# First layer's scale and shift as column-group products on TensorE instead of dot products on VectorE

## The chip, the cores and the metric

The kernel runs on one core of a Trainium2 chip. The metric is the device time of one execution in microseconds (us), the median of several runs. Engines: PE is TensorE (PEld its weight loads), DVE is VectorE, ACT is ScalarE, POOL is GpSimd, SP issues most of the loads.

## What is computed

Three layers over 256 positions of width 1024, all in float32: an attention layer (`nsa`), a dilated attention layer, and a block with two feed-forward parts and a gated delta mixer. Each layer is preceded by a norm whose scale and shift (and, behind it, whose gate) come from a conditioning row `c` by a large product. Cut to what the change touches:

```python
def adaln_norm(x, c, g, w_ada, b_ada):
    mod = jax.nn.silu(c) @ w_ada + b_ada            # c: (1, 1024), w_ada: (1024, 3072)
    shift, scale, gate = jnp.split(mod, 3, axis=-1)
    h = rms_norm(x, g) * (1.0 + scale[:, None, :]) + shift[:, None, :]
    return h, gate[:, None, :]

# first layer
h, gate = adaln_norm(x, c, norm_g[0], ada_w[0], ada_b[0])
u = h @ nsa_w_in[0]                                 # then the attention
```

So no column of the first layer's big product `h @ w_in` can start before the scale and shift of its 1024 features are there: 2 x 1024 dot products of length 1024, 8 MB of weights.

## The kernel before

All weights come as "units" of 1 MB (128 partitions x 2048 floats), one DMA each, issued by SP in the order in which the program fetches them (`fetch`, L235), into a ring of three buffers named `raw`. A load waits until its buffer's last reader is done. A weight unit of a product (`unit`, L241) is split by ACT into a rounded `hi` and by DVE into the rest `lo` (`split`, L218), and `part` (L288) multiplies hi and lo with the hi and lo halves of the activations, three passes a weight block, through `mm` (L208; every matmul of the kernel has its line L209).

An `ada` unit holds the weights of 256 output features, transposed so that a feature lies on a partition. DVE makes each as a dot product along the row: one `scalar_tensor_tensor` with `accum_out` over 128x1024 for every 128 features (L374), against the row silu(c) that stands in all partitions (`scrow`, made by `silu_row` with two PE broadcasts); one small addition adds the bias (L377). `ada_gen` is a generator, `self.step(n)` runs n units of it.

The stretch of the change is `first` (L713). It goes through the 1024 features in four steps u = 0 to 3 of 256 features. Each step runs two `ada` units (shift and scale of these 256 features), forms `a` = (1 + scale) g (L725), applies the norm to two 128-feature blocks (`apply_to`: DVE L597, ACT L600, DVE L601), and multiplies them with one weight unit, 48 matmuls of 128x256 on PE into four PSUM banks. After u = 1 and u = 3 comes one more unit (48 matmuls) for further columns. That makes 14 units: in each step two `ada` units and a weight unit, and the two extra ones. When the last step is through, the evacuations begin (`ev_kv` first), with copies and rotations on ACT, DVE and POOL, and the attention follows.

A scheduler sets the order of instructions on each engine beforehand; on the chip each engine runs its own list in order. PSUM has eight banks by tag: three `g`, two `s`, two `t`, one `o`; in `first` the four step accumulators take g, g, g, s, the extra columns s and t.

The trace also holds another stretch that the prediction reads: the compression of keys and values, L843 to L862. There `o` <- `raw`,`ke` is a float32 product with 32 columns of PE for each of eight 128-row blocks, in four column groups (`p = slice(32 * (m % 4), ...)`), `hidt` is its copy out of PSUM, and `t` <- `id`,`hidt` folds the four groups into one with a small matmul. A float32 matmul shows as two PE instructions.

Of the kernel before, what the change touches and what calls it, by code (L numbers as in the profile page):

```python
# [11 lines left out]
AF = mybir.ActivationFunctionType  # L12
ALU = mybir.AluOpType
# [130 lines left out]
def pack_units(inp, plan):  # L144

    ws = np.zeros((NUNIT, 128, 2048), np.float32)
    assert len(plan) == NUNIT
    for u, (kind, name, idx, a, b, cols) in enumerate(plan):
        w = np.asarray(inp[name])[idx]
        if kind == "gemm":  # L150
            blk = np.concatenate([w[a * 128:(a + b) * 128, c0:c0 + wd] for c0, wd in cols], 1)
            n = blk.shape[1]
            ws[u, :, :b * n] = blk.reshape(b, 128, n).transpose(1, 0, 2).reshape(128, b * n)
        elif kind == "ada":
            ws[u] = w[:, a:a + 256].T.reshape(2, 128, 1024).transpose(1, 0, 2).reshape(128, 2048)
        else:
            ws[u] = w.reshape(16, 128, 256)[a:a + 8].transpose(1, 0, 2).reshape(128, 2048)
    return ws


class Net:
    def __init__(self, ctx, tc, A, out):
        self.tc, self.nc, self.A, self.out = tc, tc.nc, A, out
        self.n = 0
        self.plan = []
        self.fine = 0
        self.queue, self.ready, self.later = [], None, []
        self.layer = "n"
        self.want32 = False
        self.rate, self.credit = RN[0], -0.25  # L170
        self.C, self.sect = {}, {}
        P = lambda name, bufs, **kw: ctx.enter_context(tc.tile_pool(name=name, bufs=bufs, **kw))
        self.cp = P("cp", 1)
        self.praw = P("praw", 3)
        self.phi = P("phi", int(2*2048//HW))
        self.plo = P("plo", int(2*2048//HW))
        self.big = P("big", 11)
        self.tmp = P("tmp", 2)
        self.ps = P("ps", 1, space=PSUM)
        self.dram = P("dram", 1, space=bass.MemoryType.DRAM)  # L180
# [182 lines left out]
    def ada_gen(self, jobs):  # L363
        nc = self.nc
        sc2 = None
        for name, idx, sc, mod, j, us, bias in jobs:
            if sc is None:
                sc = sc2 = sc2 or self.silu_row(self.A["c_2"])
            for u in us:
                raw = self.fetch("ada", name, idx, j * 1024 + u * 256, 0, None)  # L370
                for k in range(2):
                    r = raw[:, k * 1024:(k + 1) * 1024]
                    n = j * 8 + 2 * u + k
                    nc.vector.scalar_tensor_tensor(r, r, 1.0, sc, op0=ALU.mult, op1=ALU.mult, accum_out=mod[:, n:n + 1])  # L374
                if u == us[-1]:
                    o = slice(j * 8 + 2 * us[0], j * 8 + 2 * u + 2)
                    nc.vector.tensor_tensor(mod[:, o], mod[:, o], bias[:, o], op=ALU.add)  # L377
                    self.done.add((id(mod), j))
                yield

    def step(self, n=1):
        for _ in range(n):
# [11 lines left out]
    def setup(self):  # L394
        nc, A = self.nc, self.A
        v8 = lambda x: x.rearrange("p (k t) -> p k t", k=8)
        self.small = self.t(self.cp, [128, NSMALL])
        self.eps = self.t(self.cp, [128, 1])
        nc.vector.memset(self.eps, EPS)
        self.eps2 = self.t(self.cp, [128, 1])  # L400
        nc.vector.memset(self.eps2, EPS * EPS)
        self.ones = self.t(self.cp, [128, 128])
        nc.vector.memset(self.ones, 1.0)
        c = self.b8()[0:1, :1024]
        nc.sync.dma_start(c, A["c"])
        x = self.b8()
        self.xT = v8(x)
        nc.sync.dma_start(self.xT, A["xT"])
        self.consts(self.cp, "base")
        sq = self.b8()  # L410
        for h in range(2):
            nc.scalar.activation(sq[:, h * 1024:(h + 1) * 1024], x[:, h * 1024:(h + 1) * 1024], AF.Square)
        sc = self.silu_row(c, True)
        nc.sync.dma_start(self.small, A["small"])

        self.mod = [self.t(self.cp, [128, 24]), self.t(self.cp, [128, 24]), self.t(self.cp, [128, 72])]
        jobs = []
        ab, b2 = self.vec("ada_b"), self.vec("b_ada_2")
        all4 = range(4)
        for l in range(2):  # L420
            js = [(j, [u]) for u in all4 for j in range(2)] + [(2, all4)] if l == 0 else [(j, all4) for j in range(3)]
            jobs += [("ada_w", l, sc, self.mod[l], j, us, ab[:, l * 24:l * 24 + 24]) for j, us in js]
        jobs += [("w_ada_2", 0, None, self.mod[2], j, all4, b2) for j in range(9)]
        self.done = set()
        self.bg = self.ada_gen(jobs)
        self.ident, self.one = self.C["ident"], self.ones
        for n in (1024, 512, 256)[:2]:
            nc.vector.tensor_tensor(sq[:, :n], sq[:, :n], sq[:, n:2 * n], op=ALU.add)
        n //= 256
        self.ss, f = self.bank("o"), None  # L430
        for kt in range(n):
            for q in range(2):
                i = self.mm(self.ss[:, q:q + 1], sq[:, kt * 256 + q * 128:kt * 256 + q * 128 + 128], self.ones[:, 0:1], f is None, kt == n - 1, f)
                f = f or i
        self.og = self.t(self.cp, [128, 8, 2])
        self.mhalf = self.t(self.cp, [128, 16])
        nc.vector.memset(self.mhalf, -0.5)

    def silu_row(self, row, pe=False):

        nc = self.nc
        sc = self.t(self.cp, [128, 1024], tag="scrow")
        if not pe:
            nc.sync.dma_start(sc, row.to_broadcast([128, 1024]))
        for h in range(2):
# [5 lines left out]
            th = self.w([128, 512], tag="w5", bufs=4)  # L451
# [261 lines left out]
    def first(self, xT, W, ca, cb, cc, evacs):  # L713

        nc = self.nc
        mod, g = self.mod[0], self.vec("norm_g")
        r = self.rstd()
        h = [self.b8(F32R).rearrange("p (k t) -> p k t", k=8) for _ in range(2)]
        act = [(h[0][:, k], h[1][:, k]) for k in range(8)]
        a = self.w([128, 8], tag="acol")  # L720
        G = [self.group(512, tags=t) for t in ("gg", "gs", "st")]
        for u in range(4):
# [7 lines left out]
            if u in FD:  # L730
                cols = list(ca) + [cb]
                raw = self.fetch("gemm", W[0], W[1], 2 * u, 2, cols)
                for i in range(2):
                    self.direct(G[i], [raw[:, k * 1024 + i * 512:k * 1024 + i * 512 + 512] for k in range(2)], self.x32, 2 * u, 8)
            else:
                self.fine, self.last_sq = 1, None
                ws = self.unit(W, 2 * u, 2, list(ca) + [cb])
                for i in range(2):
                    c = slice(i * 512, (i + 1) * 512)
                    self.part(G[i], ws[i::2] if HW < 1024 else [(hi[:, c], lo[:, c]) for hi, lo in ws], act, 2 * u, 8, u < 3)  # L740
            if u % 2:
                if u // 2 in FC:
                    raw = self.fetch("gemm", W[0], W[1], 4 * (u // 2), 4, [cc])
# [3 lines left out]
                    self.part(G[2], ws, act, 4 * (u // 2), 8)  # L747
            if u == 2:
                self.consts(self.sp, "rope")
        for G, ev in zip(G, evacs):  # L750
            ev(G[0])
        return act

    def _nsa(self, xT):
# [3 lines left out]
        mod = self.mod[0]  # L758
# [150 lines left out]
        nc.vector.tensor_tensor(pc, pc, mx[:, :, :, None].to_broadcast([128, 2, 16, 16]), op=ALU.mult)  # L909
        self.fill(FN[5])  # L910
        self.step(AN[5])
        pct = self.w([128, 2, 256], tag="pct", bufs=1)
        b = self.bank("t")
        for g in range(2):
            for q in range(2):
# [790 lines left out]
```

## Time and profile before

| | us |
|---|---|
| median of 3 runs | 1101.57 |
| lowest and highest run | 1100.72, 1111.84 |
| the profiled execution | 1111.95 |
| span of its trace | 1110.2 |

| engine | busy us | share of the span |
|---|---|---|
| PE | 1055.9 | 95% |
| PE weight loads | 982.6 | 89% |
| DVE | 850.9 | 77% |
| ACT | 608.5 | 55% |
| POOL | 77.4 | 7% |

These shares are over the whole span; the stretch `first` is its first 62 us. Times in the rows below count from the start of the span. "Idle before" an instruction, in square brackets, is how long its engine stood still ahead of it, and what released it. The column PEclk is the granted TensorE clock, 1.00 being 2.4 GHz and 0.50 being 1.2 GHz.

### The profile page before, as it was taken

Reading aid. Unit: us, or ns where it says so; the run is one execution under the profiler, and the core shown is the slowest. Engines: PE = TensorE matmul, PEld = TensorE weight load, DVE = VectorE, ACT = ScalarE, POOL = GpSimd, SP = SyncE. Lnnn points to the kernel's source line nnn. Section 1 sums busy time; section 2 is a strip of 40 time slices with the busy share of each in tenths; the row PEclk is TensorE's granted clock in tenths of the full one; section 3 lists DMA queues with packets and bytes.
Section 4 is the critical chain, followed back from the end, with each engine's and each line's share of the span. In section 5 each row is a group of like instructions: output and inputs, shape, how many; then the busy total and the mean of one; then the engine's idle time right before and its main releaser. Section 6 shows DMA issues by size and latency. Waiting matters only on the chain.

```text
span 1110.2 us, 20852 instructions
## 1 busy us (share of the span) xinstructions
PE 1055.9 (95%) x8453; PEld 982.6 (89%) x8453; DVE 850.9 (77%) x1558; ACT 608.5 (55%) x1160; POOL 77.4 (7%) x94
## 2 busy tenths in 40 slices
PE   5879999989999999999999899999999999999997
PEld 4868767877789899999989788988899999999997
DVE  7987997998999998877798876678666776655543
ACT  3483776787665644544487256526445565444442
POOL 0030000221000000000003121310010000000000
PEclk9988999999999999999999889999899999999999
DMA  8965575575967588887744524273356545555451
GB/s 315 337 226 206 190 265 180 189 241 200 322 223 299 184 297 302 296 301 275 285 153 146 121 84 145 83 221 113 101 173 223 187 156 162 180 191 170 172 190 38
DMA packets 34577, 225.99 MB, mean 204 GB/s; under 512 B 4897, under 2 KB 5185, under 8 KB 8498
## 3 DMA queue, kind: packets, MB, share of 16 engines
q1 hardware_dynamic: 31826, 219.88, 55.7%
q0 software_dynamic: 2368, 4.27, 1.9%
q8 instruction: 66, 1.08, 0.4%
q10 hardware_dynamic: 288, 0.52, 0.1%
q14 instruction: 29, 0.24, 0.1%
HBM read 223.34 MB, written 1.31 MB: 202 GB/s over the span
## 4 chain that ended last, share of the span: by engine, by line
issue 35%; PE 24%; ACT 3%; DVE 3%; DMA 1%; POOL 0%; POOLq 0%; DVEq 0%; ACTq 0%; SPq 0%
PE g L209 17%; PE s L209 5%; PE t L209 2%; PE o L209 1%; DVE w L1241 1%; DMA raw<-in_ws_dram 1%; ACT hi L219 1%; DVE lo L222 1%; DMA b<-dr 0%; ACT d L1322 0%; ACT b L599 0%; ACT b L600 0%; ACT d L1347 0%; PE t L216 0%; DVE xt L1395 0%
## 5 line engine op out<-in xcount | busy, mean ns | idle before, releaser
L209 PE MATMUL g<-b,hi 128*128 128x256 f32 (+2 forms) x3696 | 697.5, 287 | 13.7 <-ACT b L600 8.5
L209 PEld LDWEIGHTS g<-b,hi 128*128 128x128 f32 (+1 forms) x3696 | 581.3, 191 | 22.6 <-ACT b L600 10.4
L209 PE MATMUL g<-b,lo 128*128 128x256 f32 (+2 forms) x1848 | 520.8, 287 | 4.3 <-DVE lo L222 4.2
L219 ACT CAST hi<-raw 128x1024 fp32r<-128x1024 f32 (+2 forms) x302 | 279.9, 953 | 250.7 <-PE g L209 127.1
L222 DVE TENSOR_TENSOR lo<-raw,hi 128x1024 fp32r<-128x1024 f32 (+2 forms) x302 | 329.5, 1113 | 92.4 <-ACT hi L219 89.8
L209 PEld LDWEIGHTS g<-b,lo 128*128 128x128 f32 (+1 forms) x1848 | 350.2, 192 | 8.2 <-DVE lo L222 6.6
L374 DVE SCALAR_TENSOR_TENSOR raw<-raw,scrow 128x1024 f32<-128x1024 f32 x120 | 144.8, 1227 | 8.0 <-DMA raw<-in_ws_dram 7.7
L209 PE MATMUL s<-b,hi 128*128 128x256 f32 (+1 forms) x288 | 64.0, 288 | 2.3 <-ACT w L560 2.3
L209 PE MATMUL s<-b,b 128*128 128x128 f32 (+2 forms) x224 | 49.7, 345 | 7.7 <-ACT w L691 3.1
L209 PE MATMUL g<-b,raw 128*128 128x256 f32 x208 | 52.7, 394 | 0.0
L209 PEld LDWEIGHTS s<-b,hi 128*128 128x128 f32 x288 | 49.5, 194 | 2.5 <-ACT w L560 2.5
L209 PEld LDWEIGHTS g<-b,raw 128*128 128x128 f32 x208 | 39.1, 198 | 5.9 <-issue 1.2
L209 PEld LDWEIGHTS s<-b,b 128*128 128x128 f32 x224 | 30.3, 192 | 15.1 <-issue 5.0
L1241 DVE SCALAR_TENSOR_TENSOR w<-pad,u,w 128x256 f32<-128x256 f32 x96 | 41.5, 476 | 1.0 <-ACT w L1236 0.9
L209 PE MATMUL s<-b,lo 128*128 128x256 f32 (+1 forms) x144 | 40.3, 287 | 0.0
L502 POOL TENSOR_TENSOR rcol<-rcol,u 128x2 f32<-128x2 f32 x5 | 3.5, 700 | 489.2 <-ACT rcol L501 489.2
L209 PE MATMUL t<-b,hi 128*128 128x256 f32 x160 | 37.5, 281 | 0.0
L1152 DVE TENSOR_TENSOR w<-w,g 128x512 f32<-128x512 f32 (+1 forms) x21 | 14.2, 674 | 24.8 <-PE g L209 24.8
L947 ACT ACTIVATE p<-s,mxs 128x256 f32<-128x256 f32 (+1 forms) x64 | 26.5, 422 | 7.9 <-DVE dens L950 6.6
L1150 ACT ACTIVATE w<-g 128x512 f32<-128x512 f32 (+1 forms) x21 | 12.3, 587 | 31.8 <-PE g L209 31.8
L209 PE MATMUL g<-hi,b 128*128 128x512 f32 (+1 forms) x96 | 28.7, 376 | 0.2 <-ACT w L691 0.2
L209 PEld LDWEIGHTS t<-b,hi 128*128 128x128 f32 x160 | 28.4, 188 | 0.0
(330 smaller groups left out, 1273.0 us busy)
## 6 DMA issues: line engine op xcount, KB each, us to landing
raw<-in_ws_dram SPq DMA_DIRECT2D x202, 1024.0 KB, 5.0
raw<-in_ws_dram SPq DMA_DIRECT2D x4, 512.0 KB, 5.3
b<-dr POOLq DMA_DIRECT2D x8, 256.0 KB, 6.6
raw<-in_ws_dram SPq DMA_DIRECT2D x2, 608.0 KB, 4.2
b<-in_xT_dram SPq DMA_DIRECT2D x1, 1024.0 KB, 4.9
b<-dr POOLq DMA_DIRECT2D x8, 128.0 KB, 4.1
u<-in_consts_dram SPq DMA_DIRECT2D x2, 384.0 KB, 5.0
b<-dr POOLq DMA_DIRECT2D x4, 192.0 KB, 10.1
```

What stands on the lines that cost most here:

```text
L209: i = self.nc.tensor.matmul(out, lhsT=lhsT, rhs=rhs, start=start, stop=stop, skip_group_check=True)
L219: i = self.nc.scalar.copy(hi, src)
L222: self.nc.vector.tensor_tensor(lo, src, hi, op=ALU.subtract)
L374: nc.vector.scalar_tensor_tensor(r, r, 1.0, sc, op0=ALU.mult, op1=ALU.mult, accum_out=mod[:, n:n + 1])
L502: nc.gpsimd.tensor_tensor(r, r, self.mhalf[:, 0:2], op=ALU.pow)
L947: nc.scalar.activation(p[:, br], sv[:, br], AF.Exp, bias=mx[:, q, br:br + 1], accum_out=den[:, q, br:br + 1])
L1150: nc.scalar.activation(t, gb, AF.Tanh, scale=0.5)
L1152: nc.vector.tensor_tensor(t, t, ub, op=ALU.mult)
L1241: nc.vector.scalar_tensor_tensor(dst, fl(pad[:, o:o + 256]), taps[i], dst, op0=ALU.mult, op1=ALU.add)
```

## The change

The eight `ada` units that `first` runs are no longer dot products on DVE. Their weights are packed the other way round (`adac`: the 1024 inputs on the partitions, in eight blocks, 256 output features along the row). silu(c) is put into a column tile `c4`: eight blocks of 32 columns, zero but for the first column of each. Eight float32 matmuls with `c4`'s blocks as the 32-column operand sum into four column groups of a PSUM bank `cbank` (m = 0..3 start the groups, m = 4..7 add to them). ACT copies the 128x256 result into SBUF (`hidt`), two matmuls against a column of ones fold the four groups and turn 256 features onto the partitions, into other columns of the same bank, and DVE adds the bias from there. The bank `cbank` is one of the two `t` banks. The row `scrow` is still made, since later units need it, but behind the first sum of squares.

```diff
         elif kind == "ada":
             ws[u] = w[:, a:a + 256].T.reshape(2, 128, 1024).transpose(1, 0, 2).reshape(128, 2048)
+        elif kind == "adac":
+            ws[u] = w[:, a:a + 256].reshape(8, 128, 256).transpose(1, 0, 2).reshape(128, 2048)
...
             for u in us:
+                if self.c4 is not None and len(us) == 1:
+                    self.ada_product(name, idx, mod, j, u, bias)
+                    self.done.add((id(mod), j))
+                    yield
+                    continue
                 raw = self.fetch("ada", name, idx, j * 1024 + u * 256, 0, None)
...
+    def ada_product(self, name, idx, mod, j, u, bias):
+
+        raw = self.fetch("adac", name, idx, j * 1024 + u * 256, 0, None)
+        b, n = self.cbank, j * 8 + 2 * u
+        for m in range(8):
+            p = slice(32 * (m % 4), 32 * (m % 4) + 32)
+            self.mm(b[p, :256], self.c4[:, m], raw[:, m * 256:(m + 1) * 256], m < 4, m >= 4, self.clast)
+        t = self.t(self.sp, [128, 256], tag="hidt", bufs=1)
+        self.nc.scalar.copy(t, b[:, :256])
+
+        for k in range(2):
+            self.clast = self.mm(b[:, 256 + n + k:257 + n + k], t[:, k * 128:(k + 1) * 128], self.ones[:, 0:1])
+        self.nc.vector.tensor_tensor(mod[:, n:n + 2], b[:, 256 + n:258 + n], bias[:, n:n + 2], op=ALU.add)
...
-        sc = self.silu_row(c, True)
         nc.sync.dma_start(self.small, A["small"])
+        sc = self.t(self.cp, [128, 1024], tag="scrow")
...
         n //= 256
+        self.silu_row(c, True, sc)
         self.ss, f = self.bank("o"), None
...
         act = [(h[0][:, k], h[1][:, k]) for k in range(8)]
+
+        c4, th = self.w([128, 512], tag="pct", bufs=1)[:, :256], self.w([128, 8], tag="acol")
+        self.c4 = c4.rearrange("p (k i) -> p k i", k=8)
+        nc.gpsimd.memset(c4, 0.0)
+        nc.scalar.activation(th, self.vec("c"), AF.Tanh, scale=0.5)
+        nc.vector.tensor_scalar(th, th, 1.0, 0.5, op0=ALU.add, op1=ALU.mult)
+        nc.vector.tensor_tensor(self.c4[:, :, 0], th, self.vec("c"), op=ALU.mult)
+        self.cbank, self.clast = self.bank("t"), None
         a = self.w([128, 8], tag="acol")
...
+        self.c4 = None
         for G, ev in zip(G, evacs):
```

What the scheduler makes of it on PE at the start of the program, behind the sums of squares (`o_113`), before the change (`o_135` is the norm factor spread over all partitions, `g_141` and `g_142` two of the accumulators of step u = 0):

```order
L209 MATMUL o_113<-u_4_83,b_8_91 128x1 x4
L209 MATMUL o_135<-u_7_89,rcol_132 128x128 x2
L209 MATMUL g_141<-b_30_138,hi_168 128x256 x2
L209 MATMUL g_142<-b_30_138,hi_168 128x256 x2
L209 MATMUL g_141<-b_30_138,lo_169 128x256 x2
```

and in the changed kernel at the same place (`t_146` is `cbank`, `pct_140` is `c4`, `raw_154` and `raw_169` the two units of step 0, `u_4_83` the ones):

```order
L212 MATMUL o_113<-u_4_83,b_8_91 128x1 x4
L212 MATMUL t_146<-raw_154,pct_140 32x256
L212 MATMUL o_135<-u_7_89,rcol_132 128x128 x2
L212 MATMUL t_146<-raw_154,pct_140 32x256 x7
L212 MATMUL t_146<-u_4_83,hidt_164 128x1 x2
L212 MATMUL t_146<-raw_169,pct_140 32x256 x8
L212 MATMUL t_146<-u_4_83,hidt_179 128x1 x2
L212 MATMUL g_148<-b_30_138,hi_195 128x256 x2
```

Twenty matmuls of the two units now stand on PE ahead of the first matmul of step 0, seven of the first eight products behind `o_135`.

PE at the border of steps 0 and 1, before the change (`hi_249` is the first half of step 1's weight unit):

```order
L209 MATMUL g_143<-b_31_139,hi_174 128x256 x2
L209 MATMUL s_144<-b_31_139,hi_174 128x256 x2
L209 MATMUL g_141<-b_30_138,hi_249 128x256 x2
L209 MATMUL g_142<-b_30_138,hi_249 128x256 x2
L209 MATMUL g_141<-b_30_138,lo_250 128x256 x2
```

and in the changed kernel (`raw_255` and `raw_270` are the two units of step 1, `hi_296` the first half of its weight unit):

```order
L212 MATMUL g_150<-b_31_139,hi_201 128x256 x2
L212 MATMUL s_151<-b_31_139,hi_201 128x256 x2
L212 MATMUL t_146<-raw_255,pct_140 32x256 x8
L212 MATMUL t_146<-u_4_83,hidt_265 128x1 x2
L212 MATMUL t_146<-raw_270,pct_140 32x256 x8
L212 MATMUL t_146<-u_4_83,hidt_280 128x1 x2
L212 MATMUL g_148<-b_30_138,hi_296 128x256 x2
```

All products of step 1's units stand behind the last matmul of step 0 and ahead of the first of step 1; the borders to steps 2 (there behind the 48 matmuls of the extra unit) and 3 look the same.

DVE ahead of step 1, before the change (L374 the dot products, L377 the bias, L725 `a`, L597 the norm's application, L222 the split):

```order
L222 TENSOR_TENSOR lo_175<-raw_166,hi_174 128x512 x2
L374 SCALAR_TENSOR_TENSOR raw_228,u_14_108<-raw_228,scrow_94 128x1024 x2
L377 TENSOR_TENSOR u_14_108<-u_14_108,u_1_78 128x2
L374 SCALAR_TENSOR_TENSOR raw_233,u_14_108<-raw_233,scrow_94 128x1024 x2
L377 TENSOR_TENSOR u_14_108<-u_14_108,u_1_78 128x2
L725 SCALAR_TENSOR_TENSOR acol_140<-u_14_108,u_1_78 128x2
L597 SCALAR_TENSOR_TENSOR xr_239<-b_6_87,acol_140,o_135 128x256
```

and in the changed kernel (L401 the bias, L756 `a`, L620 the application, L225 the split):

```order
L225 TENSOR_TENSOR lo_202<-raw_193,hi_201 128x512 x2
L401 TENSOR_TENSOR u_10_96<-t_146,u_1_78 128x2
L225 TENSOR_TENSOR lo_297<-raw_294,hi_296 128x512
L401 TENSOR_TENSOR u_10_96<-t_146,u_1_78 128x2
L225 TENSOR_TENSOR lo_297<-raw_294,hi_296 128x512
L756 SCALAR_TENSOR_TENSOR acol_147<-u_10_96,u_1_78 128x2
L225 TENSOR_TENSOR lo_303<-raw_294,hi_302 128x512
L620 SCALAR_TENSOR_TENSOR xr_286<-b_6_87,acol_147,o_135 128x256
```

The dot products are gone, and splits of step 1's weight unit have moved up between the bias and the application. At step 2 all splits stand ahead of the bias, at step 3 one stands behind the second bias. On SP three loads of constants (0.94 MB together) that came behind the last unit of `first` now stand ahead of step 3's three units and the extra one.

## Rows read from the trace of the kernel before

**Rows 1.** Busy time in stretches of the program: steps 0 to 3, then the rest

```profile
core 0: us, PE busy (x) PEld busy (x) DVE busy (x) ACT busy (x) POOL busy (x), PEclk, DMA share, GB/s
17.50:26.80 9.30, 8.43 (x49) 8.23 (x49) 9.16 (x20) 3.10 (x7) 0.00 (x0) 1.00 0.83 314
26.80:39.30 12.50, 11.78 (x96) 11.43 (x96) 11.54 (x22) 5.04 (x9) 0.00 (x0) 1.00 0.96 364
39.30:48.60 9.30, 6.14 (x48) 5.79 (x48) 9.16 (x20) 3.10 (x7) 0.00 (x0) 1.00 0.90 344
48.60:54.10 5.50, 5.39 (x25) 4.64 (x26) 5.47 (x11) 3.82 (x6) 0.00 (x0) 0.69 0.75 255
...
66.00:100.00 34.00, 26.73 (x193) 21.28 (x193) 27.30 (x46) 21.63 (x42) 5.22 (x5) 0.80 0.68 240
100.00:1110.00 1010.00, 978.65 (x7936) 915.70 (x7934) 768.13 (x1405) 556.19 (x1068) 65.44 (x79) 0.98 0.56 196
```

**Rows 2.** The chain that ended last, in order of time: its longest piece

```profile
907.47 195.46 issue
```

**Rows 3.** DVE in order of time ahead of step 1: start, duration, instruction

```profile
20.44 1.22 DVE L374 SCALAR_TENSOR_TENSOR raw<-raw,scrow 128x1024 f32<-128x1024 f32 x1
...
25.33 0.16 DVE L377 TENSOR_TENSOR u<-u,u 128x2 f32<-128x2 f32 x1
...
26.51 0.69 DVE L222 TENSOR_TENSOR lo<-raw,hi 128x512 fp32r<-128x512 f32 x1
```

**Rows 4.** PE in order of time: the first matmuls of steps 0 to 3

```profile
17.52 1.23 PE L209 MATMUL g<-b,hi 128*128 128x256 f32 x4 [2.07 <-ACT b L600]
...
26.80 0.74 PE L209 MATMUL g<-b,hi 128*128 128x256 f32 x4 [0.84 <-ACT b L600]
...
39.34 0.74 PE L209 MATMUL g<-b,hi 128*128 128x256 f32 x4 [0.76 <-ACT b L600]
...
48.62 0.39 PE L209 MATMUL g<-b,hi 128*128 128x256 f32 x1 [3.13 <-ACT b L600]
```

**Rows 5.** ACT in order of time: the norm ahead of step 1, a weight unit's first cast

```profile
26.24 0.91 ACT L600 ACTIVATE b<-xr,u 128x256 fp32r<-128x256 f32 x2
...
47.12 0.62 ACT L219 CAST hi<-raw 128x512 fp32r<-128x512 f32 x1 [5.87 <-DMA raw<-in_ws_dram]
```

**Rows 6.** Busy time in a stretch of 2 us, columns as in rows 1

```profile
18.00:20.00 2.00, 2.00 (x11) 2.00 (x11) 2.00 (x5) 1.42 (x3) 0.00 (x0) 1.00 1.04 434
```

**Rows 7.** PE in order of time: small matmuls of the start and the compression, one pause

```profile
11.21 1.87 PE L209 MATMUL o<-u,b 128*128 128x1 f32 x8 [5.14 <-DVE b L428]
14.23 1.22 PE L209 MATMUL o<-u,rcol 128*128 128x128 f32 x4 [1.15 <-POOL rcol L502]
...
67.61 1.07 PE L209 MATMUL o<-raw,ke 128*32 128x256 f32 x16 [1.58 <-DMA raw<-in_ws_dram]
...
74.97 1.93 PE L209 MATMUL o<-raw,ke 128*32 128x256 f32 x14
...
85.51 0.58 PE L209 MATMUL g<-b,lo 128*128 128x256 f32 x1 [1.24 <-DVE lo L222]
...
95.91 0.53 PE L209 MATMUL t<-id,hidt 128*128 128x32 f32 x4
```

**Rows 8.** ACT, costliest groups by shape: one copy of 128x256 out of PSUM

```profile
L970 ACT COPY b<-o 128x256 f32<-128x256 f32 x8 | 3.0, 376 | 5.2 <-PE o L209 5.1
```

**Rows 9.** PE alone in stretches: busy time, granted clock, DMA, in the compression

```profile
67.00:68.00 1.00, 0.39 (x8) 1.00 0.00 0
...
75.00:76.00 1.00, 1.00 (x12) 0.50 0.08 25
...
84.50:85.00 0.50, 0.00 (x0) 0.54 0.93 197
...
86.00:91.00 5.00, 5.00 (x25) 0.50 0.73 270
```

More of the change, by code (lines that the diff above doesn't have):

```diff
@@ L437, in setup, with silu_row @@
         nc.vector.memset(self.mhalf, -0.5)
-    def silu_row(self, row, pe=False):
+    def silu_row(self, row, pe=False, sc=None):
         nc = self.nc
-        sc = self.t(self.cp, [128, 1024], tag="scrow")
+        sc = self.t(self.cp, [128, 1024], tag="scrow") if sc is None else sc
         if not pe:
@@ L749, in first @@
                 self.consts(self.sp, "rope")
+        self.c4 = None
         for G, ev in zip(G, evacs):
@@ L911, in _nsa @@
         self.step(AN[5])
-        pct = self.w([128, 2, 256], tag="pct", bufs=1)
+        pct = self.w([128, 512], tag="pct", bufs=1).rearrange("p (g t) -> p g t", g=2)
         b = self.bank("t")
```

## The prediction

> **What bounds the kernel now.** I read the busy time by stretches first. From 100 us to the end PE is busy 978.65 of 1010 us [rows 1], and the longest piece of the chain of waits there is "issue" for 195.46 us [rows 2]: PE waits for nothing else. A shift of what comes before 100 us is therefore passed on to the end, and the change is worth what it does to `first`.
>
> In `first` two engines share the limit. DVE is busy 9.16 of 9.30 us in step 0 and 9.16 of 9.30 in step 2 [rows 1]: four dot products take 20.44 to 25.33 [rows 3]. PE is busy 8.43, 11.78 and 6.14 us in the same stretches and stands still only 0.84 us ahead of step 1, 0.76 ahead of step 2 and 3.13 ahead of step 3 [rows 4], because DVE's dot products run beside PE's matmuls of the step before. The loads come third: in the one wait for a weight unit shown, at 47.12, ACT stood still 5.87 us [rows 5], and the stretch moves 314 to 364 GB/s, where 434 are reached in 18 to 20 us [rows 1, 6].
>
> So PE has some 5 us of idle time at the borders of steps 0 to 3, and the reader should ask what is put into PE's list, and where.
>
> **What is removed.** Sixteen dot products, 4.9 us of DVE a step [rows 3], 19.6 us in all. They were hidden from PE but for the gaps above; what can come back from them is at most these gaps, 0.84 + 0.76 + 3.13 = 4.7 us, and the start.
>
> **What is added at a border.** By the order on PE, the products of a step's two units stand behind the previous step's last matmul, and each unit is a chain of its own: eight products, copy on ACT, fold on PE, bias on DVE. The first bias is ahead of the second unit's products, since both are in one bank. All of it is paid with PE's list held:
> - Eight products: the compression has the same shape, 128x32 weights against 128x256 in float32; sixteen PE instructions take 1.07 us at 67.61, where the granted clock is 1.00, and fourteen 1.93 us at 74.97, where it is 0.50 [rows 7, 9]. I take 1.0.
> - The copy: 0.376 us [rows 8], and two hand-overs of some 0.1: the first of two norm instructions ends at 26.24 + 0.91 / 2 = 26.70 [rows 5], PE starts on it at 26.80 [rows 4]. That is 0.55 to 0.6; I take 0.55.
> - The fold: four PE instructions, 0.53 us [rows 7]. I take 0.5.
> - The bias: 0.16 us [rows 3] and a hand-over: 0.25.
> - From the second bias to the first matmul: 25.33 to 26.80 [rows 3, 4] is 1.47, as before.
>
> Sum: (1.0 + 0.55 + 0.5 + 0.25) + (1.0 + 0.55 + 0.5 + 0.05) + 1.47 = 5.9 us. At step 1 two splits of 0.65 us (start to start; 0.69 alone, [rows 3]) stand in DVE's list between the bias and the application, at step 3 one: 7.2, 5.9 and 6.5 us in place of 0.84, 0.76 and 3.13. That is +6.4, +5.1 and +3.4, together **+14.9 us**.
>
> What is queued behind: the step's whole PE list, and the split's buffers. A product that comes later frees its `raw` buffer later, but the unit that then loads has a step of 12 us and more (5.9 to 7.2 and 6.14) ahead of it, so loads do not decide; the 0.95 MB of constants ahead of step 3's units cost 2.2 us of loading at 434 GB/s [rows 6] and are covered by the same time. If that cover were gone they would cost these 2.2 us. The zeroing of `c4`, its three small operations and the later `scrow` lie under the first loads.
>
> **The start.** `o_135` ends at 14.23 + 1.22 = 15.45 [rows 7], then seven products: fourteen instructions, to 17.4 if they take the slow 1.93 us. I take the slow durations up to step 0, since its 49 matmuls take 8.43 us against 6.14 for step 2's 48 [rows 1], though the clock column reads 1.00 for both. Copy 0.55; fold at the slow clock, half of the 1.87 us that eight instructions with one column took [rows 7], 0.93; bias 0.25; eight products 2.2; copy 0.55; fold 0.93; 0.05 and the 1.47 to the first matmul: 24.3 us, where it was 17.52 [rows 4]. **+6.8 us.**
>
> **The clock.** Step 0 took 8.43 us against 6.14 in step 2 [rows 1]. PE will have been active on and off since 11 us when step 0 starts at 24.3, so part of that loss goes: between 0 and 2.3 us, I take **-1.2**, as the last splits on DVE still end some 3.5 us behind the step's start. Step 3's first 25 matmuls took 5.39 us at a granted clock of 0.69 [rows 1], behind the 3.13 us pause [rows 4]. With the new borders PE never pauses as long: its pauses are 0.55, 0.25, 0.55 and 1.5 us. If the clock holds, step 3 gains 5.39 - 25 x 0.128 = **-2.2 us**. But in another place the clock fell in the course of a pause of only 1.24 us [rows 7], to 0.54 and 0.50, and 25 matmuls took 5.0 us instead of 3.2 [rows 9]; the pattern at the new borders is between the two. A fall costs 1.8 to 2.2 us, and there are three borders. I take one fall: **+2**.
>
> The Trainium skill (TensorE: Matmul & The Clock Gate, "A second HAM failure mode: psum-queue depth-cycling") says that short pauses of PE between groups of matmuls make the clock go back and forth between its two levels. If that held at every border, the sum would be 26, as the second rival says; the fall at 84.5 us agrees with it.
>
> **Sum.** 14.9 + 6.8 - 1.2 - 2.2 + 2 = **+20.3 us**. Behind `first` the evacuations start when the first group of step 3 is done; all engines wait for that, so the shift goes on. Against the profiled execution's 1111.95 us that is 1132; the shown runs' median is 1101.57, 0.9% below it, and as the sum is a difference I add it to the median: **1122 us**.
>
> **Rivals.**
> 1. *The loads decide, and they get faster* (the other side, not slower). Buffers that products read free early, the loads run without pauses: 17.5 to 48.6 us moved 9.3 x 314 + 12.5 x 364 + 9.3 x 344 = 10.7 MB [rows 1], 24.6 us at 434 GB/s [rows 6] in place of 31.1. Less 2.2 for the constants, a gain of 4.3: **1097 us**. For it: DVE's full stretches, ACT's 5.87 us wait. Against it: it needs the products to pass PE before the step that stands ahead of them, and PE's order has them behind. It decides only if a border's chain fits into the old gaps of 0.8 to 3.1 us; I get 5.9 to 7.2. Chance 0.05.
> 2. *The clock falls at every border.* Then step 0 and step 3 gain nothing, and steps 1 and 2 lose some 2.2 us each: 14.9 + 6.8 + 4.4 = +26, and with the products and folds there also at 0.50 (+0.9 and +0.4 a unit, six units) up to +34: **1128 to 1135 us**. Chance 0.20.
> 3. *The shift is partly absorbed.* Between 66 and 100 us PE is idle 34 - 26.7 = 7.3 us [rows 1]. If that idle time ends with loads or DVE work that do not move with `first`, or if a border's pieces overlap better than in series, up to 8 us come back and the clock holds: +8 to +12, **1110 to 1113 us**. Against it: the work there starts from step 3's accumulators. Chance 0.12.
> 4. *The four column groups do not run at once*, so that the change doesn't do what it says: sixteen instructions one after the other at no less than step 2's 0.128 us are 2.05 us in place of 1.0, eight times: +8 more, **1130 us** and up. Against it, the compression's 1.07 us [rows 7]. Chance 0.03.
>
> The Trainium skill (TensorEngine Tiling (Array Packing), "PSUM Bottleneck") warns that column groups speed up PE but not the copy out of PSUM, which may become the limit. The rows agree: the products take 1.0 us a unit, the copy and fold behind them 1.05 and more. By it alone (products free, the rest in series) a border would still cost 3.9 to 5.2 us.
>
> **How the numbers follow.** The forecast's own case, +13 to +25, has 0.60. The range leaves out rival 1, the top of 2, the upper part of 4 and the bottom of 3: 1110 to 1132. About 1% is what a measurement of this kernel can tell from no change, 11 us: faster than 1090.5 needs more than the loads give in rival 1, 0.03 of its 0.05; within 1% are the rest of it and most of rival 3, 0.12; slower than 1112.6 the rest, 0.85.
>
> **What the new profile would show.** Right: PE starts step 0 near 24 us, step 1 near 39, step 2 near 57 and step 3 near 69, with pauses released by ACT (the copy), DVE (the bias) and ACT (the norm) at each border; DVE idle in `first` for a third of the time and more; loads below 300 GB/s there; the same PE work from 100 us on, later by some 20 us. Wrong: pauses of PE that end with a load (then buffers, not the chain, decide), products that take over 2 us a unit at the granted 1.00, step 3 started before 60 us, or a shift at step 3 that is gone by 110 us. The clock's part can be read from the granted clock at the borders: 1.00 throughout takes 2 us off, 0.50 in each puts 6 on.

## The result

The changed kernel is slower: 1129.99 us median of 4 executions (1124.64 to 1134.24) where the kernel before has 1102.17 (1100.72 to 1111.84, 4 executions). The ratio is 1.0247, with a 95% interval of 1.0202 to 1.0292. Forecast were 1122 us and a range of 1110 to 1132. The sign and the mechanism came as forecast; the size was 1.8% forecast and 2.5% measured, in the upper part of the range.

The executions of one kernel lie far apart (before: 1095.29 to 1113.62 us in all sets here, changed: 1122.05 to 1134.63). So below, times in `first` are compared by one marker: the start of PE's first `g<-hi,b 128x304` matmul, the first of the stage behind step 3. Before it stands at 62.53 us, after at 85.25: **+22.7 us**.

First PE's matmuls of the changed kernel in order of time: start, duration, instructions, and in brackets the pause ahead of them and what ended it.

```profile
17.79 1.01 PE L212 MATMUL t<-u,hidt 128*128 128x1 f32 x4 [0.48 <-ACT hidt L397]
19.12 1.93 PE L212 MATMUL t<-raw,pct 128*32 128x256 f32 x16 [0.32 <-DVE u L401]
21.54 1.01 PE L212 MATMUL t<-u,hidt 128*128 128x1 f32 x4 [0.49 <-ACT hidt L397]
24.13 1.44 PE L212 MATMUL g<-b,hi 128*128 128x256 f32 x5 [1.57 <-ACT b L623]
...
31.88 1.07 PE L212 MATMUL t<-raw,pct 128*32 128x256 f32 x16
33.50 0.61 PE L212 MATMUL t<-u,hidt 128*128 128x1 f32 x4 [0.55 <-ACT hidt L397]
34.43 1.07 PE L212 MATMUL t<-raw,pct 128*32 128x256 f32 x16 [0.32 <-DVE u L401]
35.99 0.61 PE L212 MATMUL t<-u,hidt 128*128 128x1 f32 x4 [0.49 <-ACT hidt L397]
39.12 1.22 PE L212 MATMUL g<-b,hi 128*128 128x256 f32 x4 [2.52 <-ACT b L623]
...
51.92 1.07 PE L212 MATMUL t<-raw,pct 128*32 128x256 f32 x16
...
58.15 0.74 PE L212 MATMUL g<-b,hi 128*128 128x256 f32 x4 [1.57 <-ACT b L623]
...
65.54 1.07 PE L212 MATMUL t<-raw,pct 128*32 128x256 f32 x16
...
72.30 0.39 PE L212 MATMUL g<-b,hi 128*128 128x256 f32 x1 [2.05 <-ACT b L623]
...
85.25 0.30 PE L212 MATMUL g<-hi,b 128*128 128x304 f32 x1
```

Rows `t<-raw,pct` are a unit's eight products, `t<-u,hidt` its fold. From 31.88 to 39.12 the whole border of step 1 can be read: products, a pause until ACT's copy is done, fold, a pause until DVE's bias is done, and the same again, then the pause for the norm. The steps start at 24.13, 39.12, 58.15 and 72.30 us, where 17.52, 26.80, 39.34 and 48.62 stood before [rows 4].

The busy time in stretches of the same kernel, with the columns of [rows 1]:

```profile
24.00:32.00 8.00, 7.87 (x52) 7.74 (x56) 3.13 (x6) 2.03 (x5) 0.00 (x0) 1.00 0.61 221
32.00:39.00 7.00, 3.24 (x40) 1.76 (x37) 3.10 (x9) 3.25 (x8) 0.00 (x0) 0.97 0.70 258
...
24.00:85.25 61.25, 50.95 (x409) 46.12 (x409) 28.75 (x55) 23.37 (x45) 2.20 (x2) 0.92 0.61 220
...
122.00:1132.00 1010.00, 979.40 (x7940) 916.18 (x7939) 768.88 (x1405) 556.47 (x1068) 67.53 (x79) 0.98 0.56 196
```

DVE, which was busy 9.16 of 9.30 us in a step [rows 1], now works 28.75 of 61.25 us. PE is busy 7.87 of 8.00 us inside step 0 and 3.24 of 7.00 us at the border behind it, and the loads run at 220 GB/s. The last row answers to the last of [rows 1]: the same 1010 us of the program, 22 us later, hold 979.40 us of PE's work where it was 978.65.

The waits of 9 to 90 us, grouped: who waited for whom, us in total, times, the longest.

```profile
DVE u L401 <- PE t L212: 34.3, 8, 8.9
ACT hidt L397 <- PE t L212: 30.0, 8, 8.2
...
PE g L212 <- ACT b L623: 7.7, 4, 2.5
...
PE t L212 <- ACT hidt L397: 4.0, 8, 0.5
...
PE t L212 <- DVE u L401: 1.3, 4, 0.3
```

DVE and ACT wait for the products and folds, up to 8.9 us at a time, because these stand behind a whole step in PE's list. PE waits for the norm, the copies and the biases for 7.7 + 4.0 + 1.3 = 13.0 us, and no wait of PE in this stretch ends with a load.

### The profile page after: what moved, and what is told of

The parts are those of the page before. It is cut to its first block, busy times and chain, and to the rows that moved or that the text cites. A ratio compares the mean times of both kernels' runs of the same rounds, so it can differ in the third digit from the quotient of the medians.

```text
span 1132.5 us, 21164 instructions
## 1 busy us (share of the span) xinstructions
PE 1073.3 (95%) x8613; PEld 993.0 (88%) x8613; DVE 834.7 (74%) x1528; ACT 611.5 (54%) x1169; POOL 79.7 (7%) x95
## 4 chain that ended last, share of the span: by engine, by line
PE 43%; issue 36%; DVE 9%; ACT 8%; DMA 3%; POOL 0%; DVEq 0%; POOLq 0%; ACTq 0%; SPq 0%
PE g L212 25%; PE s L212 8%; PE o L212 4%; PE t L212 4%; DVE lo L225 2%; DMA raw<-in_ws_dram 2%; DVE raw L382 2%; ACT hi L222 2%; PE t L219 1%; ACT w L714 1%; DVE w L1273 1%; ACT b L623 1%; ACT b L622 1%; DVE w L715 1%; DMA u<-in_consts_dram 0%
## 5 line engine op out<-in xcount | busy, mean ns | idle before, releaser
L212 PEld LDWEIGHTS g<-b,hi 128*128 128x128 f32 (+1 forms) x3696 | 582.7, 192 | 22.7 <-ACT b L623 10.7
L222 ACT CAST hi<-raw 128x1024 fp32r<-128x1024 f32 (+2 forms) x302 | 280.3, 953 | 237.0 <-PE g L212 132.0
L225 DVE TENSOR_TENSOR lo<-raw,hi 128x1024 fp32r<-128x1024 f32 (+2 forms) x302 | 329.1, 1112 | 98.8 <-ACT hi L222 98.3
L382 DVE SCALAR_TENSOR_TENSOR raw<-raw,scrow 128x1024 f32<-128x1024 f32 x104 | 128.0, 1249 | 8.0 <-DMA raw<-in_ws_dram 8.0
L1184 DVE TENSOR_TENSOR w<-w,g 128x512 f32<-128x512 f32 (+1 forms) x21 | 14.2, 674 | 24.9 <-PE g L212 24.8
```

The source lines that it names most:

```text
L212: i = self.nc.tensor.matmul(out, lhsT=lhsT, rhs=rhs, start=start, stop=stop, skip_group_check=True)
L222: i = self.nc.scalar.copy(hi, src)
L225: self.nc.vector.tensor_tensor(lo, src, hi, op=ALU.subtract)
L1184: nc.vector.tensor_tensor(t, t, ub, op=ALU.mult)
```

## The experiments

The theory was that the shift is the series chain of products, copy, fold and bias, which PE's order puts between the steps, and that it is passed on to the end. The rivals: it is the loads or DVE (the products cost nothing), or it is TensorE's clock, which the new pauses bring down. The first four runs share 13 executions of the kernel before (median 1104.96 us), the others 11 (median 1101.72).

| kernel | steps 0, 1, 2, 3 start | marker | marker against before | median us | ratio to before [95%] |
|---|---|---|---|---|---|
| before | 17.52, 26.80, 39.34, 48.62 | 62.53 | | 1102.17 | |
| changed | 24.13, 39.12, 58.15, 72.30 | 85.25 | +22.7 | 1129.99 | 1.0247 [1.0202, 1.0292] |
| free | 17.40, -, -, 45.37 | 59.18 | -3.4 | 1099.45 | 0.9948 [0.9917, 0.9978] |
| half | 20.50, 32.19, 50.84, 62.97 | 76.56 | +14.0 | 1118.66 | 1.0127 [1.0064, 1.019] |
| ahead | 24.26, 37.22, -, - | 77.25 | +14.7 | 1119.17 | 1.0135 [1.0091, 1.0178] |
| double | 28.06, 45.24, 68.15, 86.16 | 99.11 | +36.6 | 1141.23 | 1.0336 [1.027, 1.0402] |
| changed, again | 22.42, 38.35, 57.51, 71.65 | 84.61 | +22.1 | 1131.67 | 1.0238 [1.0182, 1.0295] |
| warm | 24.96, 38.87, 57.94, 71.49 | 82.96 | +20.4 | 1125.12 | 1.0194 [1.0145, 1.0242] |
| dot0 | 17.35, 31.28, 52.20, 67.77 | 80.90 | +18.4 | 1117.92 | 1.0125 [1.0068, 1.0182] |

A dash stands where no pause or border sets the step apart.

### free: neither products nor dot products

```diff
-        for m in range(8):
-            ...
-            self.mm(b[p, :256], self.c4[:, m], raw[:, m * 256:(m + 1) * 256], m < 4, m >= 4, self.clast)
-        ...
-        self.nc.vector.tensor_tensor(mod[:, n:n + 2], b[:, 256 + n:258 + n], bias[:, n:n + 2], op=ALU.add)
+        self.nc.vector.tensor_tensor(mod[:, n:n + 2], raw[:, 0:2], bias[:, n:n + 2], op=ALU.add)
```

> The changed kernel with the scale and shift of the first layer left out: the eight units are loaded as before, but DVE only adds two of their columns to the bias (0.2 us a unit), so PE has no products, no folds and no waits for them. Theory A (the chain of products, copy and fold in PE's list is what costs): step 0 starts near 16 us, step 3 between 42 and 46 us (24.1 and 72.3 in the changed kernel, 17.5 and 48.6 before), the whole takes 1095 to 1099 us against 1102 before, some 30 us less than the changed kernel. Theory B (the loads decide, because the constants now stand ahead of step 3's units and buffers come free late): step 3 starts after 60 us all the same, 1115 us or more.

Measured: 1099.45 us, the marker at 59.18. Stretches (columns as in [rows 1]), then ACT's cast and PE's matmuls ahead of step 3 in order of time:

```profile
17.40:26.00 8.60, 8.60 (x51) 8.60 (x52) 5.22 (x12) 3.66 (x8) 0.00 (x0) 1.00 0.72 273
26.00:38.00 12.00, 12.00 (x103) 11.96 (x102) 7.40 (x15) 5.49 (x10) 0.00 (x0) 1.00 1.00 384
```

```profile
44.70 2.18 ACT L222 CAST hi<-raw 128x512 fp32r<-128x512 f32 x4 [0.75 <-DMA raw<-in_ws_dram]
45.37 0.91 PE L212 MATMUL g<-b,hi 128*128 128x256 f32 x3 [2.35 <-ACT hi L222]
```

Step 3 starts where Theory A put it, step 0 only at 17.40 us where 16 was expected. This is the most that a cheaper way of computing scale and shift could give with these loads and this order: 3.4 us at the marker, 5.5 us or 0.5% by the medians. Without the dot products PE is busy 12.00 of 12.00 us from 26 to 38, and the next thing late is a weight unit's load: the cast starts when it lands, at 44.70, and PE has stood still for 2.35 us when the first piece is cast. Before, DVE and PE were both near their limit; taking DVE's work away could win the small gaps only, and any work put onto PE there costs its full time.

### half: the scale by products, the shift by dot products

```diff
-                if self.c4 is not None and len(us) == 1:
+                if self.c4 is not None and len(us) == 1 and j == 1:
```

> The changed kernel, but only the scale of each step by products; its shift again by dot products on DVE, which lie under PE's step before. Theory A (chain in series): one chain a step falls out, 2.6 us at a border and 3.5 us at the start; step 0 starts near 20.6, step 3 near 60 us; 1110 to 1116 us. Theory B (loads): buffers of the shift units come free as before the change, those of the scale units as in the changed kernel, the time stays within 5 us of the changed kernel, 1124 us and more.

Measured: the marker at 76.56 and 1118.66 us, a bit more than expected. PE in order of time at two of its borders:

```profile
46.14 1.07 PE L212 MATMUL t<-raw,pct 128*32 128x256 f32 x16
...
50.84 0.83 PE L212 MATMUL g<-b,hi 128*128 128x256 f32 x4 [2.53 <-ACT b L623]
...
61.82 0.58 PE L212 MATMUL s<-b,hi 128*128 128x256 f32 x1 [1.38 <-ACT hi L222]
...
62.97 0.58 PE L212 MATMUL g<-b,hi 128*128 128x256 f32 x1 [0.36 <-ACT b L623]
```

Four chains fewer bring the marker down by 85.25 - 76.56 = 8.7 us, 2.2 for each, near the 2.55 us from one unit's products to the next's (31.88 to 34.43). On average the cost goes with the number of chains: the start is 3.6 us earlier, and the three borders are 4.30, 4.70 and 4.75 us long, together 6.5 us less; the four steps themselves take 1.4 us more, as the clock falls in them too. A pause of about 2 us behind the fold is paid at each border as soon as one chain stands there. It ends with the norm, or with the cast that stands behind the norm in ACT's list: 2.53 us at step 2, 1.38 and 0.36 at step 3.

### double: copy and fold twice

```diff
-        self.nc.scalar.copy(t, b[:, :256])
-
-        for k in range(2):
-            self.clast = self.mm(...)
+        for _ in range(2):
+            self.nc.scalar.copy(t, b[:, :256])
+            for k in range(2):
+                self.clast = self.mm(...)
```

> The changed kernel with the copy out of PSUM and the fold done twice in each unit, one behind the other (the second time into the same places). Theory A: each repetition adds 0.55 + 0.5 us at the clock of 2.4 GHz and 1.5 at 1.2 GHz to PE's list: 6 x 1.05 + 2 x 1.5 = +9 us, step 3 starts near 81 us, 1135 to 1140 us. (Five of step 1's products move ahead of step 0 in PE's list, 0.6 us less at that border.) Theory B (loads): the added chain is hidden under loads, within 3 us of the changed kernel.

Measured: the marker at 99.11 us and 1141.23 us, the marker 13.9 us behind the changed kernel's. PE in order of time at the border of step 2:

```profile
59.87 0.60 PE L212 MATMUL t<-u,hidt 128*128 128x1 f32 x4 [0.55 <-ACT hidt L398]
61.00 0.61 PE L212 MATMUL t<-u,hidt 128*128 128x1 f32 x4 [0.52 <-ACT hidt L398]
61.92 1.64 PE L212 MATMUL t<-raw,pct 128*32 128x256 f32 x16 [0.32 <-DVE u L401]
64.04 1.01 PE L212 MATMUL t<-u,hidt 128*128 128x1 f32 x4 [0.47 <-ACT hidt L398]
65.57 1.01 PE L212 MATMUL t<-u,hidt 128*128 128x1 f32 x4 [0.52 <-ACT hidt L398]
```

A second copy and fold add 61.00 - 59.87 = 1.13 us to a chain at the higher clock, eight times 9.0, and they are all paid; at the lower clock it is 65.57 - 64.04 = 1.53. The rest of the 13.9 us was not expected (step 3 starts at 86.16 us, forecast 81): the granted clock falls inside the longer border, and the second unit's products take 1.64 to 1.94 us in place of 1.07, its folds 1.01 in place of 0.61. Both parts say that everything between two steps is on the path that sets the end.

### ahead: the next step's units emitted beside this step's matmuls

```diff
-            self.step(2)
+            if u == 0:
+                self.step(2)
...
                 ws = self.unit(W, 2 * u, 2, list(ca) + [cb])
+                if u < 3:
+                    self.step(2)
```

> The changed kernel, but the units of the next step are emitted ahead of a step's matmuls, so that on PE the eight products, the fold and the next eight products stand between the matmuls of the step before and the pauses are filled with them. Theory A: a border falls from 6.2 to 7.2 us to 0.5 to 1.6, each step grows by the 3.2 us of its products and folds; step 3 starts near 62 us in place of 72; 1113 to 1119 us: the series costs some 11 us of the 27, the mere PE time of the products some 10, the start 7. Theory B (loads or buffers): PE now waits for the next step's units inside a step, with pauses that end with a load, step 3 stays near 70 us and the time at 1125 and more.

Measured: the marker at 77.25 and 1119.17 us, the upper end of Theory A's time, though step 3 starts only near 66 us where 62 was expected. The products now stand between matmuls, and the borders' chains are gone; PE's longest pauses are others (ACT's rows are the norm and the cast ahead of step 1):

```profile
35.75 0.91 ACT L623 ACTIVATE b<-xr,u 128x256 fp32r<-128x256 f32 x2 [1.67 <-DVE xr L620]
36.56 2.17 ACT L222 CAST hi<-raw 128x512 fp32r<-128x512 f32 x4
37.22 1.03 PE L212 MATMUL g<-b,hi 128*128 128x256 f32 x6 [1.43 <-ACT hi L222]
...
43.62 1.07 PE L212 MATMUL t<-raw,pct 128*32 128x256 f32 x16
...
48.70 0.39 PE L212 MATMUL s<-b,hi 128*128 128x256 f32 x1 [1.97 <-ACT hi L222]
...
49.96 0.58 PE L212 MATMUL s<-b,lo 128*128 128x256 f32 x1 [0.76 <-DVE lo L225]
```

So the place of the chain, with what it does to the clock, is worth 85.25 - 77.25 = 8.0 us; the granted clock falls once here between step 0 and the marker, at 50 us, and three times in the changed kernel. It does not bring back the time before, for two reasons that the rows show. The start, 24.26 us, has nothing ahead of it to hide behind and costs its 6.7 us as in the changed kernel. And at step 1 and behind its first 48 matmuls PE waits 1.43 + 1.97 + 0.76 us for casts and splits of weight units. No cast waits for a load in this stretch: the casts stand behind the norm in ACT's list, and the norm waits for the bias of the chain, so the cast of step 1 starts at 36.56, as the norm ends. The six later units still cost PE's time for products and folds, 1.07 + 0.61 by the modelled rows, even where they stand beside other work.

### dot0: step 0's two units by dot products, as before

```diff
-                if self.c4 is not None and len(us) == 1:
+                if self.c4 is not None and len(us) == 1 and u > 0:
```

> The changed kernel with step 0's two units made by dot products on DVE again, the other six by products. Theory A (the start costs 6.8 us, since both units' chains stand ahead of step 0): step 0 starts at 17.5 us, step 1 near 33.5, step 3 near 67, all 5.5 to 7 us ahead of the changed kernel, 1120 to 1124 us. Theory B (the start is covered by the wait for the first weight unit): step 0 starts no earlier than 20 us or step 1 waits for its units instead, and less than 3 us are gained.

Measured: step 0 starts at 17.35 us again, the marker stands at 80.90 and the median is 1117.92 us, below what was expected. The start's term is 24.13 - 17.35 = 6.8 us; of it 4.4 are left at the marker. The steps in between ran at a low clock for longer in this execution, as in step 1, which starts at 31.28 (PE alone by stretches: length, busy time, granted clock, DMA share, GB/s):

```profile
34.00:36.00 2.00, 2.00 (x12) 0.50 0.65 225
36.00:38.00 2.00, 2.00 (x13) 0.63 0.81 295
```

The clock is still at its lower level 5 us behind the start of the step; in the changed kernel it is back at 1.00 some 3 us behind it. The four steps take 43.05 us together, 2.2 more than the changed kernel's 40.89.

### warm: matmuls without a result in PE's pauses

```diff
+        for i in range(2):
+            self.mm(self.obank[:, 256:512], self.ones, raw[:, i * 256:i * 256 + 256])
         for k in range(2):
...
+        for i in range((1, 5)[j]):
+            self.mm((self.obank if j == 0 else b)[:, 288:512], self.ones, t[:, :224])
...
```

> The changed kernel with matmuls whose results nobody reads put into PE's pauses at the borders: two of 128x256 during each copy, one or four of 128x224 behind each fold. Theory A, clock part: PE does not pause, the granted clock stays at 1.00, steps 1 to 3 take 5.8 to 6.2 us each for their first 48 matmuls (7.2 to 7.4 in the changed kernel) and step 3's first group ends 2 us earlier; with 0.2 us that an added matmul may overhang in each pause it comes to 3 to 5 us less than the changed kernel, stage behind step 3 from 80 to 82.5 us. Theory B (the clock has no part in the 27 us): the same time or up to 3 us more.

Measured: the marker at 82.96 us, 0.5 us above what was expected, and 1125.12 us, 6.5 below the changed kernel in the same set. PE alone by stretches, columns as above; first the changed kernel in step 0 and at its borders, then *warm*, and *warm*'s products and added matmuls in order of time.

```profile
26.00:28.00 2.00, 2.00 (x11) 1.00 0.00 0
...
36.00:38.00 2.00, 0.60 (x4) 1.00 1.00 393
38.00:40.00 2.00, 0.88 (x4) 0.65 0.85 360
40.00:42.00 2.00, 2.00 (x11) 0.50 0.75 184
...
60.00:62.00 2.00, 2.00 (x11) 0.50 0.99 410
...
74.00:76.00 2.00, 2.00 (x12) 0.50 0.42 170
```

```profile
40.00:42.00 2.00, 2.00 (x20) 1.00 1.02 426
...
74.00:76.00 2.00, 2.00 (x19) 1.00 0.08 18
```

```profile
30.82 1.07 PE L212 MATMUL t<-raw,pct 128*32 128x256 f32 x16
31.82 1.13 PE L212 MATMUL o<-raw,u 128*128 128x256 f32 x4
...
50.43 1.07 PE L212 MATMUL t<-raw,pct 128*32 128x256 f32 x16
...
63.85 1.07 PE L212 MATMUL t<-raw,pct 128*32 128x256 f32 x16
```

In the changed kernel the clock is at its lower level, 0.50, for 3 to 4 us at every border: 11 or 12 matmuls in 2 us, where *warm* runs 19 or 20. A step ends where the next products start; *warm*'s four steps take 5.86 + 11.56 + 5.91 + 11.47 = 34.80 us and the changed kernel's 7.75 + 12.80 + 7.39 + 12.95 = 40.89. So the clock costs 6.1 us in the steps: 1.9 in step 0, which is behind the start, and 4.2 in steps 1 to 3, behind the three borders, 1.4 for each. The net gain at the marker is 2.3 us, because the added matmuls overhang: two with 256 columns take 1.13 us, more than the copy's pause of 0.55, and the borders become 8.05, 7.5 and 7.6 us long.

### The two kernels once more

> The changed kernel once more, timed in more rounds. In the first trace of it the second product stage behind step 3 starts 22.7 us later than before (85.25 against 62.53 us), and nothing behind that differs; the first timing gave +27 us with an interval of 22 to 32. If the shift is passed on one to one: 1.018 to 1.024 times the kernel before. If something behind it costs more: 1.025 and up again.

> The kernel before once more, for its trace: executions of it lie between 1099 and 1114 us, and its first trace belongs to one of 1112. If the difference lies in the granted clock behind 100 us, a faster execution shows the same steps in the first 62 us and fewer stretches at 0.50 later; if it lies in the first 62 us, the shift of the changed kernel has to be taken against another start.

Measured: the kernel before gave 1111.36 us with the marker at 62.49, so that no trace here shows a faster execution of it; the changed kernel gave 1131.67 us (1122.05 to 1134.63) with the marker at 84.61 in the profiled execution. That execution, of 1122.85 us, is 11.4 us shorter than the one profiled first (1134.24), but its marker is only 0.6 us earlier. Its start was 1.7 us earlier, but its steps took 0.7 us more and its borders 0.4. Most of the difference lies in one place far behind `first`, where some 8 us are lost by ACT's instructions matched one by one, and the rest in smaller falls behind 790 us; PE alone by stretches, the changed kernel's first profile and then its second:

```profile
652.00:662.00 10.00, 8.58 (x25) 0.55 0.00 1
662.00:672.00 10.00, 10.00 (x89) 0.77 0.00 0
```

```profile
652.00:662.00 10.00, 10.00 (x103) 1.00 0.00 1
```

The kernel before shows the same fall in its profiled execution, 22 us earlier:

```profile
630.00:640.00 10.00, 8.70 (x25) 0.53 0.01 2
```

So this fall is in executions of both kernels. From marker to the end of the span the first profiles take 1047.7 us (before) and 1047.2 us (changed), both with the fall: the shift in `first` is passed on whole. The second profile of the changed kernel takes 1036.5 us for the same stretch, and the altered kernels' between 1032.7 (*double*) and 1047.0 (*dot0*).

## Why the prediction was right, and where it was off

- **What bounds the kernel.** Right. The same PE work stands behind 100 us, later by the shift, and nothing is absorbed: 1047.7 and 1047.2 us from marker to end in the two profiles with the same late fall. The medians of the six altered kernels, against the kernel before in their own set, moved as their markers did, within 3 us: half +13.7 (marker +14.0), ahead +14.2 (+14.7), double +36.3 (+36.6), free -5.5 (-3.4), dot0 +16.2 (+18.4), warm +23.4 (+20.4).
- **The borders.** Right: 7.24, 6.23 and 6.76 us (31.88 to 39.12, 51.92 to 58.15, 65.54 to 72.30), forecast 7.2, 5.9 and 6.5; over the old gaps +15.5, forecast +14.9. The pieces came as priced, but for the fold, 0.61 us where 0.5 was taken, and the wait for the bias, 0.32 where 0.25 was.
- **The start.** Right: 24.13 us, +6.6, forecast 24.3 and +6.8. In the second profile it was 22.42, 1.9 less than forecast, since the first fold and the second unit's products there ran at the faster durations (0.61 and 1.07 us, where the first profile has 1.01 and 1.93).
- **The clock.** This is the step that was mis-sized. Forecast was -1.2 - 2.2 + 2 = -1.4 us, with one fall at three borders. The clock fell at all three, and the four steps together take 40.89 us where they took 8.44 + 11.78 + 6.15 + 13.91 = 40.28: +0.6. By *warm* the three falls cost 4.2 us, 1.4 each: three falls in place of one, each cheaper than the 2 us taken, so that the two errors cancel in part, which is luck. The last pause of a border was 2.52, 1.57 and 2.05 us; the prediction's 1.5 left out the splits that its own sum for the borders had in it. Without the falls the other two terms were near: *warm*'s steps 1 to 3 are 2.9 us shorter than before (forecast 2.2 for step 3), and step 0 of the changed kernel gained 0.7 (forecast 1.2). Of the two prices named for the borders, 2 us off with the clock at 1.00 throughout was near (2.7: steps 1 to 3 take 28.94 us in *warm*, and 31.6 with the forecast's one fall), and 6 us on with 0.50 in each does not: the clock fell in each, and the sum was only 2.4 us above the forecast.
- **The sum.** +22.7 us at the marker (6.6 + 15.5 + 0.6), forecast +20.3. The difference is the clock's 2.0 us, the borders' 0.6 and -0.2 at the start.
- **From the sum to the median.** The medians lie 27.8 and 30.0 us above those before in their own sets, the ratios say +27 and +26, and the markers +22.7 and +22.1. So 4 to 8 us of the measured difference were not forecast and do not lie in `first`; both intervals (+22 to +32 and +20 to +33) still hold the markers' shift, so that this rest is not clear of noise. It does not lie in the work behind `first` either where the two profiles with the same late fall are compared (spans 1110.2 and 1132.5, 22.3 apart). That the clock falls more often behind `first` in the changed kernel's executions is possible, since the time from marker to end differs by up to 15 us between the profiles here, but was not shown: both traces of the kernel before are of its longer executions. It stays open.
- **Rival 1, the loads decide.** Refuted. No pause of PE in 24 to 85 us of the changed kernel ends with a load, and the border chains are no shorter than forecast. *free* shows what was in it: 3.4 us, where the rival had 4.3.
- **Rival 2, the clock falls at every border.** Its mechanism came true and its price did not. Steps 1 and 2 lost 1.0 and 1.2 us, not 2.2 each, steps 0 and 3 gained 0.7 and 1.0, and the products inside the borders stayed at 1.07 us in the first profile. Its time, 1128 to 1135, holds both measured medians, while the forecast's 1122 is 8 us below the first; but its sum of +26 to +34 is not what the marker shows, +22.7. The Trainium skill (TensorE: Matmul & The Clock Gate, "A second HAM failure mode: psum-queue depth-cycling") tells of a clock that changes level because PE idles briefly between groups of matmuls; the trace agrees, with 0.50 behind pauses of 0.32 to 2.52 us at all three borders.
- **Rival 3, the shift is absorbed behind `first`.** Refuted by the 1047.7 and 1047.2 us.
- **Rival 4, the column groups run in turn.** Refuted: sixteen PE instructions of a unit take 1.07 us, as in the compression [rows 7]. The Trainium skill (TensorEngine Tiling (Array Packing), "PSUM Bottleneck") says that packing speeds up the matmul but not the way out of PSUM; here, of the 2.55 us from one unit to the next, 1.48 are the copy, the fold and the bias.

## What to carry to other kernels

An engine at 98% busy is not the bound if another one waits for it only a little: before moving its work, leave the work out and see what the kernel gains (0.5% here), because the second engine may be as full. Work that is moved onto the engine which sets the end is paid in full, and a chain that goes engine to engine (products, copy, fold, bias) is paid with all its hand-overs when the order puts it between two groups of matmuls. Emitting it beside the group ahead took back 8.0 of 22.7 us, a part of it by fewer falls of the clock, but the price of the products themselves and of what stands at the start remains.

## What was not expected of the hardware

- At each of the three borders the granted clock fell to 0.50 behind pauses of PE of 0.32 to 0.55 us with a last one of 1.57 to 2.52 us. In the first profile the products and folds between these pauses still ran at 1.00 durations; the low level took the next step's first matmuls, for 3 to 4 us.
- At the start the same kernel ran at either level in two executions: the first fold took 1.01 us in one and 0.61 in the other, and step 0 began at 24.13 and 22.42 us. The clock column does not show it: it reads 1.00 in the first profile's step 0 (26 to 28 us), where 11 matmuls run in 2 us, as many as at 0.50 behind a border (40 to 42 us). So for the start the durations have to be read and not the column, as the prediction did.
- A fold of four PE instructions with one column each takes 0.61 us at 1.00 and 1.01 at 0.50 (*double*, 64.04), more than half of the eight products with 256 columns (1.07 and, at the slow start, 1.93).
- A late fall, behind 630 us (before) or 652 us (changed), is there in one profiled execution of the changed kernel and not in the other. The two are 11.4 us apart, some 8 of them there.
